# Up projections of a decoder trunk: the last product into the first accumulator with both operand parts at once, and a group's first two weight blocks rounded together

## The chip, the cores and the metric

The kernel runs on one core of one Trainium2 chip (trn2). The metric is the device time of one execution in microseconds; the figure given for a kernel is the median of its runs. A profiled execution has its own time, which stands beside its span (first to last instruction).

The engines in the profile: PE (TensorE, the matrix products; PEld are its weight loads), DVE (VectorE), ACT (ScalarE), POOL (GpSimd) and SP (SyncE, which issues most of the DMAs). Each has a queue of its own that it works off in order.

## The reference

A decoder layer with two feed-forward networks (FFNs) around a mixer, on a sequence of 512 positions with a model width of 1024. Only the FFNs matter here:

```python
D_MODEL = 1024
SEQ = 512
D_FF = 2816

def swiglu(x, w_gate, w_up, w_down):
    return (jax.nn.silu(x @ w_gate) * (x @ w_up)) @ w_down

x = x + 0.5 * swiglu(rmsnorm(x, ffn1_norm[l]), ffn1_wg[l], ffn1_wu[l], ffn1_wd[l])
x = x + hybrid_mixer(...)
x = x + 0.5 * swiglu(rmsnorm(x, ffn2_norm[l]), ffn2_wg[l], ffn2_wu[l], ffn2_wd[l])
```

Input and output are float32. The gate and up projections (`x @ w_gate`, `x @ w_up`) are what the change touches; they stand in both FFNs.

## The kernel before

**Two-part products.** PE multiplies operands rounded to a short float format (F32R). To keep float32 accuracy the kernel splits each operand into a rounded part and what the rounding leaves: `wsplit` (line 235) makes `wh` by a copy on ACT and `wl` by a subtraction on DVE. A product is then the sum of three: rounded weights with the rounded operand, rounded weights with the operand's rest, the weights' rest with the rounded operand. A moving operand `m` of 256 columns is kept as one tile of 512: `m[:, lo]` is the rounded part, `m[:, hi]` the rest.

**Fast scheme over blocks.** `ffn_up` (line 376) makes the gate and up projections. The first columns of the weights go the direct way (in the first FFN a few blocks before it as well). The rest goes through a seven-product scheme: of a two by two split of weights and operand, seven products of half size stand for eight. The weights come in groups: a *pass* `w` takes two column blocks of the gate weights (even `w`, `o.j` = 0) or of the up weights (odd `w`). The first FFN has 16 passes, the second 18 (`count`). A pass has seven steps, numbered 1 to 7 in the code (here p1 to p7), each with its own weight block of 512 columns: raw halves of the loaded tile for p1 and p2 (`o.x`), loaded blocks or sums for the others. `s2` and `s4` are sums that `add_weights` makes on DVE.

**Order of steps.** The list `stream` (line 449) sets it: in each pass p1, p2, p4 of the pass before, p6, p3 of the pass before, p5, p7. One step is one item `i` of the stream, done in this order (the loop at the end of `ffn_up`): `products(i)` on PE, `results(i - 1)` on ACT and DVE, `prepare(i + LEAD)`, which rounds the weights of four steps ahead, and DMAs for later passes. Rounded weights live in tiles of 1024 columns that hold two consecutive steps (`units`, three of each kind). Once in 14 steps, a number of times, `halve` also rounds a finished result `h` for the down projection (`hh` on ACT, `hl` on DVE): in the first FFN six times, in the second four.

**Accumulators.** Each pass has three PSUM banks: `o.beta` (tag mm) collects p1, p6, p7 and p4 in turn, `o.gamma` (tag aux) p5 and p3, `o.p2` (tag aux) p2. After p1, p6 and p7 ACT copies what stands in beta's first half to SBUF, and the next of them goes on adding into the same bank, so PE may not start it before the copy is done. `t1` and `t2` (tiles `tg` in even passes, `tu` in odd ones) collect results; `silu` runs on them in even passes, and in odd passes DVE multiplies them with those of the even pass before, into `h`.

**Wide steps.** In `products` a step is either narrow, per weight tile three products of 256 columns (rounded weights with `m[:, lo]`, with `m[:, hi]`, and the weights' rest with `m[:, lo]`), or wide, per weight tile one product of 512 columns (rounded weights with the whole of `m`, so that the two parts land in the two halves of the bank) and one of 256. A wide step leaves a second half in the bank, which DVE has to add. `wide(p, w)` (line 504) says which: before, p2, p5 and p3, from pass `FIRST_WIDE` = 2 on, p5 and p3 not in the last two passes.

**What order holds what.** ACT and DVE work off their queues in the order in which the code emits. In a step that follows p4 (that is during p6), `results` for p4 comes first, then the rounding of the block four steps ahead, which is p1 of the next pass.

The other places that the prediction names: `psum` pools of four banks for each tag; `load` (line 432) issues a pass's loads; `halve` (line 598); the calls of `ffn_up` at lines 803 and 1698. All engine calls pass through one recording line, so the profile puts every instruction at L170, and rows are told apart by tile names: `wh<-wr` and `wh<-s` are rounding copies, `wl<-...` the subtractions, `tg<-mm` and `tu<-mm` ACT's copies out of beta, `tg<-aux` and `tu<-aux` DVE's answers to p2, p5 and p3, `mm<-cm,wh` a product into beta, `aux<-cm,wh` one into the other banks.

Of the kernel before, what the change touches and what calls it, by code (L numbers as in the profile page):

```python
# [9 lines left out]
F32 = mybir.dt.float32  # L10
F32R = mybir.dt.float32r
AF = mybir.ActivationFunctionType
# [31 lines left out]
LEAD = 4  # L44
PLAIN, PAIRS, TAIL = 6, 8, 3
DIRECT = 4
WIDE, FIRST_WIDE = (2, 5, 3), 2


ORDER = """  # L50
# [125 lines left out]
def hybrid_kernel(ctx, tc, xt, vec, w1u, w1d, wm, wki, wrg, watt, wrnn, wout, w2u, w2d, gf, out):  # L176
    nc = tc.nc
    plan = Plan()
    V, A = plan.engine("DVE", nc.vector), plan.engine("ACT", nc.scalar)
# [18 lines left out]
    def nm(s):  # L198
        cnt[0] += 1
        return f"{s}_{cnt[0]}"  # L200

    def slot(dt=F32, name="s"):
        return plan.take("slot", big.tile([P, S], dt, tag="slot", name=nm(name)))

    def work(name="t", cols=S):
        return plan.take("tmp", tmp.tile([P, cols], F32, tag="tmp", name=nm(name)))

    def awork(name="a"):
        return patt.tile([P, S], F32, tag="att", name=nm(name))

    def psum(tag="mm"):
        return psp.tile([P, S], F32, tag=tag, name=nm(tag))
# [22 lines left out]
    def wsplit(r, h, l):  # L235
        A.activation(h, r, AF.Copy)
        V.tensor_sub(l, r, f(h))
# [75 lines left out]
    lo, hi = slice(0, HS), slice(HS, S)  # L313
# [62 lines left out]
    def ffn_up(y, wu, n0, hs, g, waiting=(), given=(), ahead=None):  # L376
# [10 lines left out]
        ws = []  # L387
# [65 lines left out]
        w = count - 1  # L453
        stream[-3:] = [(5, w), (7, w), (3, w - 1), (4, w), (3, w)]
        units = []

        def add_weights(i):
            p, w = stream[i] if i < len(stream) else (0, 0)
            o = ws[w]
            if p == 6:  # L460
                o.s2 = slot(F32, "s2")
                V.tensor_add(o.s2, o.s1, o.x[:, :H])
            if p == 3:
                o.s4 = slot(F32, "s4")
                V.tensor_add(o.s4, o.s2, o.x[:, H:])

        def prepare(i):
            if i < LEAD:
                add_weights(i)
            if i + 1 >= LEAD:  # L470
                add_weights(i + 1)
            p, w = stream[i]
            o = ws[w]
            if i % 2 == 0:
                units.append([wsp.tile([P, WMAX], F32R, tag=t, name=nm(t)) for t in ("wh", "wl")])
            h, l = (t[:, i % 2 * H:(i % 2 + 1) * H] for t in units[i // 2])
            wsplit({1: lambda: o.x[:, :H], 2: lambda: o.x[:, H:], 6: lambda: o.s2, 5: lambda: o.s1, 7: lambda: o.s3,
                    4: lambda: o.a22, 3: lambda: o.s4}[p](), h, l)
# [25 lines left out]
        def wide(p, w):  # L504

            return p in WIDE and FIRST_WIDE <= w < count - 2 * (p != 2)

        def results(i):
            p, w = stream[i]
            o = ws[w]  # L510
            if p == 1:
                o.t1, o.t2 = (work("tg"), work("tg")) if o.j == 0 else (awork("tu"), awork("tu"))
                A.activation(o.t1[:, lo], o.beta[:, lo], AF.Copy)
            elif p == 2:
                V.tensor_sub(o.t1[:, lo], o.p2[:, lo], o.t1[:, lo])
                if wide(2, w):
                    V.tensor_add(o.t1[:, lo], o.p2[:, hi], o.t1[:, lo])
            elif p == 6:
                A.activation(o.t1[:, hi], o.beta[:, lo], AF.Copy)
            elif p == 7:  # L520
                A.activation(o.t2[:, hi], o.beta[:, lo], AF.Copy)
                V.tensor_add(o.t2[:, hi], o.gamma[:, lo], o.t2[:, hi])
                if wide(5, w):
                    V.tensor_add(o.t2[:, hi], o.gamma[:, hi], o.t2[:, hi])
                if o.j:
                    o.h2 = slot(F32, "h")
                    V.tensor_mul(o.h2[:, hi], o.t2[:, hi], ws[w - 1].t2[:, hi])
                else:
                    A.activation(o.t2[:, hi], o.t2[:, hi], AF.Silu)
            elif p == 4:  # L530
                if o.j:
                    V.tensor_mul(o.h2[:, lo], o.beta[:, lo], ws[w - 1].t2[:, lo])
                else:
                    A.activation(o.t2[:, lo], o.beta[:, lo], AF.Silu)
            elif p == 3:
                V.scalar_tensor_tensor(o.t1[:, hi], o.gamma[:, lo], -1.0, o.t1[:, hi], op0=ALU.mult, op1=ALU.subtract)
                if wide(3, w):
                    V.tensor_sub(o.t1[:, hi], o.t1[:, hi], o.gamma[:, hi])
                if o.j:
                    o.h1 = slot(F32, "h")  # L540
                    V.tensor_mul(o.h1, o.t1, ws[w - 1].t1)
                    hs.extend((o.h1, o.h2))
                else:
                    A.activation(o.t1, o.t1, AF.Silu)

        with tc.manual_schedule(engines=ENGINES):
# [4 lines left out]
            for d, (n, j) in enumerate(direct):  # L551
                sums.append(psum(("aux", "mm")[n % 2]))
                if d == 1:
                    norm_rest(norm)
                    hs.extend(ffn_act(*p) for p in waiting)
                gemm(sums[d], split_[d], y, range(KD), last=False, upto=KD // 2)
                steps = [results_direct(d - 1)] if d else []
                if d + 2 < len(direct):
                    together(prepare_direct(), *steps)
                    fetch()  # L560
                else:
                    together(*steps)
                    for i in range(2):
                        prepare(2 * (d + 2 - len(direct)) + i)
                if d == 0:
                    for _ in range(3):
                        next(norm)
                if d in (4, 6):
                    load_ = load(len(ws))
                if d >= 4:  # L570
                    next(load_, None)
                if d > 1:
                    next(operands, None)
                gemm(sums[d], split_[d], y, range(KD), first=False, since=KD // 2)
                if d > 1:
                    next(operands, None)
            for _ in operands:
                pass
            for i in range(len(stream)):
                products(i)  # L580
                if i:
                    results(i - 1)
                else:
                    together(results_direct(len(direct) - 1))
                if i + LEAD < len(stream):
                    prepare(i + LEAD)
                elif not ahead or i + LEAD - len(stream) < PLAIN - f0:
                    halve(hs, f0 + i + LEAD - len(stream))
                if ahead:
                    ahead(i - len(stream))  # L590
                if i % 14 == 12 and i // 14 < f0:
                    halve(hs, i // 14)
                if i % 7 == 1 and len(ws) < count:
                    load_ = load(len(ws))
                next(load_, None)
            results(len(stream) - 1)

    def halve(hs, n):
# [182 lines left out]
    def given(r):  # L781
        h, l = (wsp.tile([P, WMAX], F32R, tag=t, name=nm(t)) for t in ("wh", "wl"))
        wsplit(r, h, l)
        return h, l
# [10 lines left out]
    pu, w = psum(), given(AH[0])  # L795
# [779 lines left out]
    steps, index, units, turned, tasks_at = d2.steps, d2.index, d2.units, d2.turned, d2.tasks_at  # L1575
# [211 lines left out]
```

## Time and profile before

| | us |
|---|---|
| median of three runs | 1067.38 (1066.7 to 1067.38) |
| the profiled execution | 1067.44 |
| its span | 1065.6 |
| PE busy | 1056.1 |
| DVE busy | 879.8 |
| ACT busy | 652.8 |
| POOL busy | 155.8 |

How to read the rows. A row of the timeline has start and length in us from the start of the span, then engine, line, operation, the tile written and those read, shapes, and how many equal rows were merged (x2); in brackets the engine's idle time before it and who ended it. Lengths of consecutive rows on ACT and DVE overlap, since one starts before the last has written everything; what an engine can take is therefore read from start to start. Matmuls overlap in the same way. In the windows each engine has its busy us in that stretch and in brackets its instructions. The chain is followed back from the last instruction of the program.

The product streams lie at about 74 to 235 us (first FFN) and 765 to 945 us (second).

### The profile page before, as it was taken

How to read it: one execution, taken by the hardware profiler on the slowest of the kernel's cores; microseconds unless marked ns; L12 is line 12 of the kernel's file. 1: busy time of each engine (PE TensorE's matmuls, PEld its weight loads, DVE VectorE, ACT ScalarE, POOL GpSimd, SP SyncE). 2: the span in 40 equal slices, each digit the busy share in tenths (PEclk: the TensorE clock that was granted, in tenths of full speed). 3: DMA queues.
4: the chain of work that ended last, by engine and by line, in shares of the span. 5: the costliest groups of instructions: out<-in, count | busy, mean ns of one | idle time of the engine just before them, and what ended most of it. 6: DMA issues, size and time to landing. Idle time of an engine off the chain costs nothing.

```text
span 1065.6 us, 17037 instructions
## 1 busy us (share of the span) xinstructions
PE 1056.1 (99%) x6084; PEld 929.0 (87%) x6084; DVE 879.8 (83%) x1734; ACT 652.8 (61%) x1295; POOL 155.8 (15%) x187
## 2 busy tenths in 40 slices
PE   9999999999999999999999999999999999999997
PEld 7889999999999888888888888888899999998885
DVE  6687898889978889898989866766878988878885
ACT  6575555556656669867796573446655555565753
POOL 0161111102430000000000000001511111101610
PEclk9999999999999999999999999999999999999999
DMA  8298777738983442232223212434977786638973
GB/s 278 60 260 190 162 200 182 179 109 236 262 197 105 146 134 79 85 109 80 83 76 99 80 41 59 139 111 113 245 190 164 190 198 162 163 120 255 256 160 119
DMA packets 71701, 161.77 MB, mean 152 GB/s; under 512 B 8512, under 2 KB 14784, under 8 KB 71616
## 3 DMA queue, kind: packets, MB, share of 16 engines
q1 hardware_dynamic: 46608, 119.72, 34.8%
q0 software_dynamic: 24576, 40.38, 23.0%
q8 instruction: 48, 0.79, 0.3%
q10 hardware_dynamic: 432, 0.57, 0.1%
q14 instruction: 37, 0.30, 0.1%
HBM read 151.73 MB, written 2.10 MB: 144 GB/s over the span
## 4 chain that ended last, share of the span: by engine, by line
PE 94%; DVE 3%; ACT 2%; issue 1%; DMA 0%; SPq 0%; ACTq 0%
PE mm L170 66%; PE aux L170 28%; DVE wl L170 1%; ACT wh L170 1%; DVE ca L170 1%; DMA x<-xt 0%; ACT cm L170 0%; DVE h L170 0%; DVE cb L170 0%; DVE tg L170 0%; ACT tg L170 0%; DVE cm L170 0%; ACT yh L170 0%; SPq L158 0%; DVE o L170 0%
## 5 line engine op out<-in xcount | busy, mean ns | idle before, releaser
L170 PE MATMUL mm<-cm,wh 128*128 128x256 f32 x1472 | 268.5, 283 | 0.1
L170 PEld LDWEIGHTS mm<-cm,wh 128*128 128x128 f32 x1472 | 229.1, 191 | 3.5 <-ACT tg L170 0.3
L170 DVE TENSOR_TENSOR wl<-wr,wh 128x512 fp32r<-128x512 f32 (+2 forms) x228 | 188.7, 831 | 49.6 <-ACT wh L170 48.0
L170 ACT ACTIVATE wh<-wr 128x512 fp32r<-128x512 f32 (+3 forms) x230 | 167.9, 737 | 68.8 <-PE mm L170 23.4
L170 PE MATMUL mm<-cm,wl 128*128 128x256 f32 x736 | 208.4, 283 | 0.0
L170 PE MATMUL mm<-yh,wh 128*128 128x512 f32 (+1 forms) x416 | 164.0, 395 | 0.8 <-ACT wh L170 0.8
L170 PE MATMUL mm<-yl,wh 128*128 128x512 f32 (+1 forms) x416 | 162.3, 391 | 0.1
L170 PE MATMUL mm<-yh,wl 128*128 128x512 f32 x408 | 159.3, 390 | 0.0
L170 PE MATMUL aux<-cm,wh 128*128 128x512 f32 (+1 forms) x552 | 159.2, 351 | 0.0
L170 PEld LDWEIGHTS mm<-cm,wl 128*128 128x128 f32 x736 | 140.4, 191 | 0.0
L170 ACT ACTIVATE wh<-s 128x512 fp32r<-128x512 f32 x152 | 92.9, 624 | 54.3 <-DVE s L170 41.8
L170 DVE TENSOR_TENSOR wl<-s,wh 128x512 fp32r<-128x512 f32 x152 | 103.5, 686 | 24.9 <-ACT wh L170 23.2
L170 PE MATMUL aux<-cm,wl 128*128 128x256 f32 x440 | 123.8, 281 | 0.0
L170 PEld LDWEIGHTS aux<-cm,wh 128*128 128x128 f32 x552 | 96.6, 189 | 12.5
L170 PEld LDWEIGHTS mm<-yh,wh 128*128 128x128 f32 (+1 forms) x416 | 77.9, 187 | 17.6 <-ACT wh L170 1.4
L170 PEld LDWEIGHTS mm<-yl,wh 128*128 128x128 f32 (+1 forms) x416 | 77.6, 187 | 15.7 <-DVE yl L170 0.8
L170 PEld LDWEIGHTS mm<-yh,wl 128*128 128x128 f32 x408 | 76.6, 188 | 16.6 <-DVE wl L170 0.2
L170 PEld LDWEIGHTS aux<-cm,wl 128*128 128x128 f32 x440 | 83.5, 190 | 0.0
L170 PE MATMUL mm<-wh,cm 128*128 128x512 f32 x192 | 59.0, 389 | 0.0
L170 ACT ACTIVATE tg<-tg 128x512 f32<-128x512 f32 (+1 forms) x44 | 24.1, 548 | 50.8 <-DVE tg L170 50.7
L158 POOL DMA_DIRECT2D cm<-cb x8 | 7.1, 884 | 320.4 <-PE mm L170 265.6
L158 POOL DMA_DIRECT2D s<-w2u x36 | 33.5, 1063 | 125.9 <-DMA s<-w2u 42.2
(243 smaller groups left out, 2049.5 us busy)
## 6 DMA issues: line engine op xcount, KB each, us to landing
wr<-wm SPq DMA_DIRECT2D x39, 512.0 KB, 3.6
wr<-w2u SPq DMA_DIRECT2D x26, 512.0 KB, 5.1
wr<-w1u SPq DMA_DIRECT2D x21, 512.0 KB, 5.6
wr<-w1d SPq DMA_DIRECT2D x18, 512.0 KB, 4.7
s<-w2u SPq DMA_DIRECT2D x36, 256.0 KB, 5.9
s<-w2u POOLq DMA_DIRECT2D x36, 256.0 KB, 5.3
wr<-w2d SPq DMA_DIRECT2D x18, 512.0 KB, 5.6
s<-w1u SPq DMA_DIRECT2D x32, 256.0 KB, 5.9
```

The costliest lines, as they stand in the source:

```text
L158: return self.engine.dma_start(out, src, **kw)
L170: return call(*args, **kw)
```

## The change

Two things, in both FFNs.

First, p4 becomes a wide step in passes 2 to `count` - 3. Its product with rounded weights covers both operand parts and lands in both halves of `beta`. `results` for such a p4 copies beta's first half to t2 on ACT, adds the second half on DVE, and only then finishes t2 as a whole: in an odd pass one product of 512 columns into `h`, in an even pass one `silu` over 512 columns. What p7's results did to t2's second half (a product of 256 or a silu of 256) is left out there.

Second, where p1 falls on an even step, which is so in pass 0 and every even pass, its block and p2's, the two halves of the loaded tile `o.x`, are rounded by one call of `wsplit` over 1024 columns when p1's turn comes, and p2's turn does nothing.

```diff
-WIDE, FIRST_WIDE = (2, 5, 3), 2
+WIDE, FIRST_WIDE = (2, 5, 3, 4), 2
...
                 units.append([wsp.tile([P, WMAX], F32R, tag=t, name=nm(t)) for t in ("wh", "wl")])
+            if p == 1 and i % 2 == 0:
+
+                wsplit(o.x, *units[i // 2])
+                return
+            if p == 2 and i % 2:
+                return
             h, l = (t[:, i % 2 * H:(i % 2 + 1) * H] for t in units[i // 2])
...
                 if wide(5, w):
                     V.tensor_add(o.t2[:, hi], o.gamma[:, hi], o.t2[:, hi])
+                if wide(4, w):
+                    return
                 if o.j:
                     o.h2 = slot(F32, "h")
                     V.tensor_mul(o.h2[:, hi], o.t2[:, hi], ws[w - 1].t2[:, hi])
                 else:
                     A.activation(o.t2[:, hi], o.t2[:, hi], AF.Silu)
+            elif p == 4 and wide(4, w):
+                A.activation(o.t2[:, lo], o.beta[:, lo], AF.Copy)
+                V.tensor_add(o.t2[:, lo], o.beta[:, hi], o.t2[:, lo])
+                if o.j:
+                    o.h2 = slot(F32, "h")
+                    V.tensor_mul(o.h2, o.t2, ws[w - 1].t2)
+                else:
+                    A.activation(o.t2, o.t2, AF.Silu)
             elif p == 4:
                 if o.j:
                     V.tensor_mul(o.h2[:, lo], o.beta[:, lo], ws[w - 1].t2[:, lo])
```

## The prediction

> **What bounds the kernel now.** I read the page first: its busy times and the shares of the chain that ended last.
>
> ```profile
> span 1065.6 us, 17037 instructions
> PE 1056.1 (99%) x6084; PEld 929.0 (87%) x6084; DVE 879.8 (83%) x1734; ACT 652.8 (61%) x1295; POOL 155.8 (15%) x187
> PE 94%; DVE 3%; ACT 2%; issue 1%; DMA 0%; SPq 0%; ACTq 0%
> ```
>
> PE is busy nearly throughout and carries 94% of the chain. Next I asked the chain for a stretch inside the product stream of the first FFN, the only kind of place that the change touches. Columns are start, length, what ran.
>
> ```profile
> 114.54 2.88 PE mm L170 x24
> ...
> 123.11 1.41 PE aux L170 x8
> ...
> 134.51 2.88 PE mm L170 x24
> ```
>
> Here every step is PE. A block of twelve 128x256 products takes 2.88 / 2 = 1.44 us, a wide one (four 128x512 and four 128x256) 1.41 us. A pass of the stream has seven blocks; two passes take 134.51 - 114.54 = 19.97 us, which is 8 x 1.44 + 6 x 1.41 = 19.98, so PE loses nothing. Who is next? The windows (busy us of each engine) and the timelines of DVE, ACT and PE in one pair of passes tell.
>
> ```profile
> 130.00:160.00 30.00, 30.00 (x218) 28.36 (x217) 27.11 (x53) 17.93 (x37) 5.96 (x7) 1.00 0.71 184
> ```
>
> ```profile
> 120.52 0.69 DVE L170 TENSOR_TENSOR s<-s,wr 128x512 f32<-128x512 f32 x1
> 121.12 0.69 DVE L170 TENSOR_TENSOR wl<-a,wh 128x512 fp32r<-128x512 f32 x1
> ...
> 122.92 0.88 DVE L170 TENSOR_TENSOR tg<-aux,tg 128x256 f32<-128x256 f32 x2
> 124.81 1.48 DVE L170 TENSOR_TENSOR wl<-s,wh 128x512 fp32r<-128x512 f32 x2 [1.01 <-ACT wh L170]
> 126.21 0.88 DVE L170 TENSOR_TENSOR tu<-aux,tu 128x256 f32<-128x256 f32 x2
> 127.00 0.68 DVE L170 TENSOR_TENSOR wl<-s,wh 128x512 fp32r<-128x512 f32 x1
> 127.60 1.47 DVE L170 TENSOR_TENSOR wl<-wr,wh 128x512 fp32r<-128x512 f32 x2
> 128.99 0.42 DVE L170 SCALAR_TENSOR_TENSOR tg<-aux,tg 128x256 f32<-128x256 f32 x1
> 129.44 0.42 DVE L170 TENSOR_TENSOR tg<-tg,aux 128x256 f32<-128x256 f32 x1
> 129.78 0.69 DVE L170 TENSOR_TENSOR s<-s,wr 128x512 f32<-128x512 f32 x1
> 131.08 0.69 DVE L170 TENSOR_TENSOR wl<-a,wh 128x512 fp32r<-128x512 f32 x1 [0.62 <-ACT wh L170]
> ```
>
> ```profile
> 123.83 0.42 ACT L170 ACTIVATE tg<-tg 128x256 f32<-128x256 f32 x1 [1.61 <-DVE tg L170]
> ...
> 126.00 0.38 ACT L170 ACTIVATE tg<-mm 128x256 f32<-128x256 f32 x1
> 126.28 0.62 ACT L170 ACTIVATE wh<-wr 128x512 fp32r<-128x512 f32 x1
> 127.44 0.39 ACT L170 ACTIVATE tu<-mm 128x256 f32<-128x256 f32 x1 [0.54 <-PE mm L170]
> ...
> 129.89 0.63 ACT L170 ACTIVATE tg<-tg 128x512 f32<-128x512 f32 x1 [1.55 <-DVE tg L170]
> 130.43 0.61 ACT L170 ACTIVATE wh<-a 128x512 fp32r<-128x512 f32 x1
> ```
>
> ```profile
> 122.95 0.40 PE L170 MATMUL aux<-cm,wh 128*128 128x512 f32 x1
> ...
> 130.06 0.40 PE L170 MATMUL mm<-cm,wh 128*128 128x256 f32 x2
> ```
>
> DVE is 90% busy (27.11 of 30), and it follows: block p2 of this pass begins at 122.95 and its answer, tu<-aux, at 126.21, 3.26 us later. DVE runs its rows strictly in order, so a row that waits holds all behind it.
>
> **DVE's budget per pair of passes, before.** Spacings, start to start: a 512 row 0.60 us (120.52 to 121.12); two dependent 256 rows 0.79 (126.21 to 127.00); a 256 row 0.45 if the next needs it (128.99 to 129.44), else 0.34 (129.44 to 129.78). From the code a pair holds 14 roundings (8.40), four sums of weights (2.40), two pairs on t1's first half (1.58), on t2's second half 0.79 and 1.24 (the odd pass adds a product), the odd pass's product with t2's first half 0.34, on t1's second half 0.79 and, with the odd pass's 512 product, 1.50, and one rounding of an earlier h (0.60): 17.64. To that come two waits that recur every pair, since DVE feeds ACT's silu and then waits for the rounding copy behind it: before 124.81, 124.81 - 122.92 - 0.79 = 1.10; before 131.08, 131.08 - 129.78 - 0.60 = 0.70. Together 19.44, against PE's 19.97. DVE has 0.53 us to spare per pair, not the 10% that its busy share suggests.
>
> **The change part by part.** *Wide p4 on PE.* It applies to passes 2 to count-3: 12 of 16 in the first FFN, 14 of 18 in the second. Each turns a 1.44 block into a 1.41 block: 26 x 0.03 = 0.78 us less. That is all that PE can gain.
>
> *The extra add and the longer product (DVE).* The beta bank now has a second half to be added. Even pass: one 256 row, 0.34 more. Odd pass: 0.45 for the add plus 0.60 for one 512 product, in place of 0.34 and 0.45 for two 256 ones: 0.26 more.
>
> *Silu of t2 moves.* Before, the even pass ran silu on t2's second half between DVE's adds and the p3 rounding, which is the 1.10 wait; that goes. Its first half came straight from the bank (tg<-mm, 126.00) and asked nothing of DVE. Now ACT copies the half out, waits for DVE's add, runs silu over 512, and only then does the next rounding copy, for which DVE waits. Queued behind ACT's silu are that rounding and then tu<-mm (127.44), the copy that empties the next pass's bank.
>
> *Merged rounding.* In every even pass's p1 and p2 one 1024 copy and one 1024 subtraction stand for two of 512. The direct products already have such rows:
>
> ```profile
> 744.32 1.04 ACT L170 ACTIVATE wh<-wr 128x1024 fp32r<-128x1024 f32 x1
> 745.27 0.71 ACT L170 ACTIVATE cm<-ca 128x256 fp32r<-128x256 f32 x2
> ...
> 745.39 1.23 DVE L170 TENSOR_TENSOR wl<-wr,wh 128x1024 fp32r<-128x1024 f32 x1 [0.53 <-ACT wh L170]
> 746.54 0.68 DVE L170 TENSOR_TENSOR h<-h,tg 128x512 f32<-128x512 f32 x1
> ```
>
> DVE: 746.54 - 745.39 = 1.15 for 1.20, 0.05 less. But the subtraction starts 745.39 - 744.32 = 1.07 after the copy starts, a 512 one 131.08 - 130.43 = 0.65 after it: 0.42 more waiting. The merge falls in the very step where ACT runs the moved silu, because an even pass's p1 is prepared four blocks ahead, in p6 of the odd pass, right behind results of p4.
>
> The Trainium skill (Perfetto Trace Analysis, Optimizing Scalar/DVE Operations) says that larger operations can raise throughput when the engine is saturated, and that splitting them can end work sooner when the engine is not saturated but others wait for it. The rows show both at once, -0.05 busy and +0.42 waiting, so by the first half of that rule alone the pair would come out 0.42 us shorter than below.
>
> *Sum for DVE after.* Busy: 17.64 + 0.34 + 0.26 - 0.05 = 18.19. Waits: the 0.70 stays; the 1.10 goes; new, from the add's start to the 1024 subtraction: add 0.42, 0.03 until silu (129.44 + 0.42 = 129.86, silu at 129.89), 0.54 until the copy (129.89 to 130.43), 1.07 until the subtraction, less the 0.34 that DVE spends on the add itself: 1.72. Total 20.61, against PE's 19.97 - 0.06 = 19.91. DVE now falls behind by 0.70 per pair; without the h rounding (made for six pairs in the first FFN, four in the second) by 0.10. Unmerged, the same sum gives 18.24 + 0.70 + 1.30 = 20.24.
>
> *Where PE feels it.* Block p7 of an odd pass overwrites the bank that tu<-mm empties. Now that copy ends at 127.44 + 0.39 = 127.83, and p7 starts at 130.06: 2.23 to spare. After, with DVE as punctual as now: add at 127.60 (where DVE is free), silu 128.05, copy of 1024 at 128.59, tu<-mm at 129.54 (0.95 later, 744.32 to 745.27), done 129.93, against 130.03. So the slack is gone before DVE is late at all. The first pairs are better off, as DVE starts ahead:
>
> ```profile
> 794.10 0.40 PE L170 MATMUL aux<-cm,wh 128*128 128x512 f32 x1
> ...
> 796.87 0.88 DVE L170 TENSOR_TENSOR tu<-aux,tu 128x256 f32<-128x256 f32 x2
> ```
>
> In pass 3 the answer to p2 comes after 2.77 us, not 3.26, and the lost 1.10 wait helps once. I set the changed order out row by row with these spacings from pass 0 (the old order set out so answers p2 after 2.72 in pass 3 and 3.20 in pass 5, and PE never waits). Spare time at p7: 1.35 in pass 3, 0.58 in pass 5, then none. PE waits 0.31 in the third pair (0.22 at p7 of pass 7, 0.09 at the next p6), and from then on about what DVE loses, 0.67 to 0.76. First FFN, six pairs: 0.31 + 0.76 + 0.76 + 0.67 = 2.50. Second, seven pairs, the last three without the h rounding: 0.31 + 0.67 + 3 x 0.16 = 1.46. Loss 3.96, gain 0.78: +3.2 us.
>
> DMA issues keep their order on both queues, and weights are fetched a pass ahead; I cost that at nothing (bound: one late landing, which would show as a wait of ACT's copy for a DMA). The down projections start with DVE about 1.5 us later than now but with blocks of plain products rounded four blocks ahead, so nothing there; without that cover, up to 1.5 per FFN, 3.0.
>
> **The number.** The profiled execution took 1067.44 us around its span of 1065.6; the median shown is 1067.38, the same to 0.01%. 1067.4 + 3.2 = 1070.6. The spacings are known to about 1.5%. Short by that, DVE's 18.19 loses 0.27 per pair, and the layout ends at +1.2; long by it, at +5.8. So this case's own range is 1068.6 to 1073.2.
>
> **Rivals.** *The cover holds.* If DVE and ACT overlap a little better than laid out, PE never waits and the wide block alone counts: 1067.4 - 0.8 = 1066.6. For it: the first two pairs need it anyway, and 0.10 per pair decides in the second FFN. Against: the 1.72 wait is a chain of measured rows. It decides if DVE's pair stays under 19.91, 0.70 less than my sum.
>
> *DVE behind from the first pair.* If nothing is gained at the start and the h rounding does not matter, all 13 pairs lose 0.70: +9.1 - 0.8, 1075.7. Against it: the 2.77 above.
>
> *The weight loads count.* The change drops 4 of 12 loads per block. If PE were paced by loads, at 1.44 / 12 = 0.12 us each, 26 x 0.48 = 12.5 us would go and the kernel would take 1054.9. The rows speak against it: wide blocks already drop those loads and take 1.41, not 0.96. The Trainium skill (TensorE: Matmul & The Clock Gate, Back-to-back issue gap) has 131 ns per N=512 product in a sustained stream; by that, as an estimate, a wide block takes 4 x 0.131 + 4 x 0.12 = 1.00 us and the change saves 26 x 0.44 = 11.4 us; the trace, with its 1.41, does not agree.
>
> **Chances.** Forecast 54%, cover holds 32%, DVE behind from the start 11%, weight loads 3%. What a measurement of this kernel can tell from no change is 0.2%, 2.1 us: faster means below 1065.3, slower above 1069.5. The forecast gives slower in 46 of its 54, the rest no change; cover holds gives no change; so faster 3%, same 40%, slower 57%. The range goes from 1066.3, just under the cover case, to 1074.6, above the long-spacing end and short of the last rival.
>
> **What would show it.** Right: PE's waits list gains ACT's tu copy (PE mm behind ACT tu) with some ten waits under 0.8 us, all in the stream's later passes; passes of a pair take 20.6 us there in the first FFN, about 20.1 late in the second; DVE waits about 1.7 us before the 1024 subtraction; blocks of p4 take 1.41. Wrong: PE gapless at 19.91 per pair (cover holds), or gaps from pass 3 on, or waits of PE for wl rather than for the bank.

## The result, and the profile after

| | before | after |
|---|---|---|
| median (us) | 1067.02 (1066.37 to 1067.38, 6 runs) | 1071.17 (1070.95 to 1071.75, 6 runs) |
| ratio, 95% interval | | 1.0039 [1.0029, 1.005] |
| span of the profiled execution (us) | 1065.6 | 1069.3 |

The change makes the kernel 4.15 us slower. The page of the kernel after, its span, its busy times and the shares of the chain:

```profile
span 1069.3 us, 16812 instructions
PE 1058.2 (99%) x5980; PEld 923.7 (86%) x5980; DVE 883.4 (83%) x1730; ACT 653.6 (61%) x1291; POOL 154.3 (14%) x187
PE 96%; ACT 1%; DVE 1%; issue 1%; DMA 0%; SPq 0%; DVEq 0%; ACTq 0%
```

There are 104 products fewer (26 steps times 4), as the change says, and no share of busy time tells where the loss is: PE reads 99% and DVE 83% in both. PE's list of waits (total us, times, longest) does:

```profile
PE mm L170 <- ACT tu L170: 1.4, 4, 0.4
PE aux L170 <- DVE epst L170: 1.1, 1, 1.1
PE aux L170 <- DVE tu L170: 1.0, 1, 1.0
PE aux L170 <- DVE acc L170: 0.2, 1, 0.2
```

The second and the fourth line stand in the list of before too. The first and the third are new: short waits for ACT's copy out of beta, and one long one for DVE. To see what each costs I divided both traces at the starts of PE's products: where each stream begins and ends, and where the second down projection has its opening part behind it (its first product with an operand of tag cm). Lengths in us; the last columns are kernels of the experiments below.

| stretch | before | after | one region | wide alone | silu later |
|---|---|---|---|---|---|
| up to the first stream | 73.80 | 73.15 | 73.11 | 73.50 | 72.85 |
| first stream | 160.54 | 162.77 | 162.81 | 161.78 | 160.32 |
| first down projection | 113.39 | 113.40 | 113.39 | 113.39 | 113.39 |
| between the FFNs | 417.65 | 417.62 | 417.63 | 417.74 | 417.63 |
| second stream | 180.86 | 182.02 | 182.03 | 181.11 | 180.64 |
| opening of the second down projection | 19.21 | 20.41 | 19.30 | 19.41 | 19.21 |
| rest | 100.19 | 99.94 | 99.93 | 99.88 | 99.91 |

Three stretches account for the loss: +2.23 in the first stream, +1.16 in the second, +1.20 behind it. Together they are 4.59; the first and the last row are 0.90 shorter, which leaves the 3.69 between the two spans. These two rows move from kernel to kernel where nothing was changed, the first by up to 0.95 and the last by up to 0.31 in the table, so I read nothing from them.

**The streams.** Around one late event of the first stream, DVE, ACT and PE of the kernel after:

```profile
185.85 1.28 DVE L170 TENSOR_TENSOR wl<-s,wh 128x512 fp32r<-128x512 f32 x2
187.05 0.88 DVE L170 TENSOR_TENSOR tu<-aux,tu 128x256 f32<-128x256 f32 x2
...
188.44 0.42 DVE L170 TENSOR_TENSOR tg<-mm,tg 128x256 f32<-128x256 f32 x1
190.51 1.23 DVE L170 TENSOR_TENSOR wl<-wr,wh 128x1024 fp32r<-128x1024 f32 x1 [1.65 <-ACT wh L170]
```

```profile
188.89 0.63 ACT L170 ACTIVATE tg<-tg 128x512 f32<-128x512 f32 x1 [2.10 <-DVE tg L170]
189.43 1.04 ACT L170 ACTIVATE wh<-wr 128x1024 fp32r<-128x1024 f32 x1
190.38 0.36 ACT L170 ACTIVATE tu<-mm 128x256 f32<-128x256 f32 x1
```

```profile
190.16 0.28 PE L170 MATMUL aux<-cm,wl 128*128 128x256 f32 x1
190.79 0.50 PE L170 MATMUL mm<-cm,wh 128*128 128x256 f32 x2 [0.35 <-ACT tu L170]
191.13 0.28 PE L170 MATMUL mm<-cm,wl 128*128 128x256 f32 x1
```

The reader is to follow one thread through the three. DVE adds p4's second half at 188.44. ACT's silu, which needs that sum, starts at 188.89; the rounding copy queued behind it at 189.43; DVE's subtraction, which needs the copy, at 190.51. Behind the same copy ACT has tu<-mm, which empties the bank that p7 is to write. It ends at 190.38 + 0.36 = 190.74, and p7 starts at 190.79, 0.63 behind the last product before it where 0.12 is usual. How often this happens shows in the chain, at the starts of p7 in the odd passes:

```profile
170.12 3.14 PE mm L170 x24
...
190.79 3.14 PE mm L170 x24
...
211.47 3.12 PE mm L170 x24
```

They are 20.67 and 20.68 us apart: that is a pair of passes now, against 19.97 before. In the second stream pairs are 20.68 while an `h` is rounded in them, and 20.07 or 20.08 later.

**Behind the second stream.** The long wait. ACT, DVE and PE of the kernel after at the end of the stream:

```profile
948.81 0.38 ACT L170 ACTIVATE xr<-mm 128x256 f32<-128x256 f32 x1 [2.75 <-PE mm L170]
949.09 0.63 ACT L170 ACTIVATE tg<-tg 128x512 f32<-128x512 f32 x1
949.62 1.14 ACT L170 ACTIVATE wh<-wr 128x512 fp32r<-128x512 f32 x2
```

```profile
950.27 0.69 DVE L170 TENSOR_TENSOR wl<-wr,wh 128x512 fp32r<-128x512 f32 x1 [2.30 <-ACT wh L170]
...
951.81 0.42 DVE L170 SCALAR_TENSOR_TENSOR tu<-aux,tu 128x256 f32<-128x256 f32 x1
```

```profile
939.54 0.49 PE L170 MATMUL mm<-ident,x 128*128 128x128 f32 x3
...
948.50 0.71 PE L170 MATMUL mm<-ident,x 128*128 128x128 f32 x5
...
952.28 0.50 PE L170 MATMUL aux<-wh,hh 128*128 128x512 f32 x1 [1.00 <-DVE tu L170]
```

The rows mm<-ident are transposes that belong to the down projection. In the kernel before, PE runs eight of them in a row behind the stream's last product, and ACT copies their results in one go:

```profile
945.44 1.03 PE L170 MATMUL mm<-ident,x 128*128 128x128 f32 x8
```

```profile
946.08 1.21 ACT L170 ACTIVATE xr<-mm 128x256 f32<-128x256 f32 x4 [0.21 <-PE mm L170]
```

In the kernel after, three of the eight run at 939.54, inside the stream, and ACT's first copy of their results, xr<-mm, stands in its queue ahead of the last silu, tg<-tg. That copy waits until PE comes to the other transposes at 948.50; silu, two rounding copies and DVE's work wait with it, and a bank that DVE has to read out comes free only at 952.2, 1.00 us late for PE. In the code of the changed kernel nothing is moved there: the stream and the down projection are two regions of hand-set order, and at the border between them the framework's scheduler orders the instructions by itself.

### The profile page after: what moved, and what is told of

Read it like the earlier page. It is cut to its first block, busy times and chain, and to the rows that moved or that the text cites. A ratio compares the mean times of both kernels' runs of the same rounds, so it can differ in the third digit from the quotient of the medians.

```text
span 1069.3 us, 16812 instructions
## 1 busy us (share of the span) xinstructions
PE 1058.2 (99%) x5980; PEld 923.7 (86%) x5980; DVE 883.4 (83%) x1730; ACT 653.6 (61%) x1291; POOL 154.3 (14%) x187
## 4 chain that ended last, share of the span: by engine, by line
PE 96%; ACT 1%; DVE 1%; issue 1%; DMA 0%; SPq 0%; DVEq 0%; ACTq 0%
PE mm L170 68%; PE aux L170 28%; ACT wh L170 1%; DMA x<-xt 0%; DVE wl L170 0%; ACT yh L170 0%; SPq L158 0%; DVE o L170 0%; DVE tg L170 0%; ACT tu L170 0%; DVE yl L170 0%; DVE xr L170 0%; DVE acc L170 0%; DVE sq L170 0%; ACT sq L170 0%
## 5 line engine op out<-in xcount | busy, mean ns | idle before, releaser
L170 PE MATMUL mm<-cm,wh 128*128 128x256 f32 (+1 forms) x1368 | 269.1, 293 | 1.5 <-ACT tu L170 1.4
L170 DVE TENSOR_TENSOR wl<-wr,wh 128x512 fp32r<-128x512 f32 (+2 forms) x211 | 185.2, 886 | 65.6 <-ACT wh L170 65.1
L170 PEld LDWEIGHTS mm<-cm,wh 128*128 128x128 f32 x1368 | 216.4, 191 | 12.4 <-ACT tu L170 4.0
L170 ACT ACTIVATE wh<-wr 128x512 fp32r<-128x512 f32 (+3 forms) x213 | 164.6, 780 | 69.8 <-PE mm L170 23.4
L170 ACT ACTIVATE tg<-tg 128x512 f32<-128x512 f32 (+1 forms) x44 | 26.9, 611 | 54.9 <-DVE tg L170 54.9
```

What stands on the lines that cost most here:

```text
L170: return call(*args, **kw)
```

## The experiments

**The border: one region around the stream and the down projection.** Everything else as in the kernel after.

```diff
+    with tc.manual_schedule(engines=ENGINES):
         ffn_up(y2, w2u, 0, hs, V_G2, ahead=tasks_at)
         with tc.manual_schedule(engines=ENGINES):
...
```

> The changed kernel, with the second FFN's product stream and its down projection ordered as one region, so that the first transposes of the down projection and ACT's copies of them stand behind the stream's last rows again, as they did before the change. Nothing else differs. Theory: the loss has two parts, DVE behind in the streams (+2.2 us in the first, +1.2 us in the second) and one wait of 1.0 us at the second down projection that comes from the changed order at the seam. Then this kernel takes 1070.1 us or a little less, the waits in the streams stay, and no PE wait of 1 us is left at the seam. Rival: the wait at the seam is DVE's lag of the stream, paid late; then it stays about 1.0 us and the time about 1071.2.

Measured 1070.09 us (1069.96 to 1070.36), 1.0029 [1.0018, 1.0041] of before. ACT's queue at the same place:

```profile
947.99 0.63 ACT L170 ACTIVATE tg<-tg 128x512 f32<-128x512 f32 x1 [1.95 <-DVE tg L170]
948.52 1.14 ACT L170 ACTIVATE wh<-wr 128x512 fp32r<-128x512 f32 x2
949.57 1.19 ACT L170 ACTIVATE xr<-mm 128x256 f32<-128x256 f32 x4
```

The silu is again ahead of the copies. In PE's list of waits the 1.0 us line is gone, the one for ACT's tu copy is still there with 1.4 us in 4 waits, and the opening takes 19.30 instead of 20.41: 1.1 of the 4.15 us came from the border. The streams are as they were (162.81 and 182.03). Why the scheduler moved the transposes in the kernel after and not in the one before wasn't tried.

**The wide step alone.** The two conditions in `prepare` for the merged rounding are taken out; with the one region, so compare with the run above.

```diff
-            if p == 1 and i % 2 == 0:
-
-                wsplit(o.x, *units[i // 2])
-                return
-            if p == 2 and i % 2:
-                return
```

> The wide p4 alone: the first two blocks are rounded one by one again; the seam ordered as one region. Theory (DVE's pair 20.24 us against PE's 19.91 while an h is rounded, 19.64 without): the first stream 1.1 us longer than before, the second about 0.1 shorter, so 1068.1 us, with PE waits of 0.2 to 0.4 us from pass 9 on in the first stream. Rival (the merged rounding helps, the wide p4 alone costs all): 1070 or more. Rival (the extra add is hidden): 1066.3.

Measured 1067.99 us (1067.7 to 1069.24), 1.0011 [1.0002, 1.002] of before, 2.1 us less than with the merge. ACT and DVE of this kernel at the event that was shown for the kernel after:

```profile
188.58 0.63 ACT L170 ACTIVATE tg<-tg 128x512 f32<-128x512 f32 x1 [2.11 <-DVE tg L170]
189.12 0.61 ACT L170 ACTIVATE wh<-wr 128x512 fp32r<-128x512 f32 x1
189.64 0.36 ACT L170 ACTIVATE tu<-mm 128x256 f32<-128x256 f32 x1
189.90 0.62 ACT L170 ACTIVATE wh<-wr 128x512 fp32r<-128x512 f32 x1
```

```profile
188.13 0.42 DVE L170 TENSOR_TENSOR tg<-mm,tg 128x256 f32<-128x256 f32 x1
189.76 1.48 DVE L170 TENSOR_TENSOR wl<-wr,wh 128x512 fp32r<-128x512 f32 x2 [1.22 <-ACT wh L170]
```

Two things are better than with the merge. DVE waits 1.22, and inside the row of two (which takes 1.40 to the next row, not 1.20) another 0.20, instead of 1.65. And tu<-mm now stands between the two copies, so it follows the start of the first by 0.52, not by 0.95. No wait of PE for it is listed any more; DVE and ACT still fall behind, only later: counted from p2 of the odd passes, pairs of the first stream take 19.95 up to pass 9, then 20.38 and 20.50, and the chain then goes through ACT's copy tg<-mm into p6. The forecast's sum for this pair was 20.24; the 0.20 inside the row of two isn't in that sum. The first stream is 1.24 longer than before, where 1.1 was expected. In the second, where the `h` rounding stops early, little is lost: 181.11 is 0.25 over the kernel before, where 0.1 under it was expected.

**The merge alone.** p4 narrow as before.

```diff
-WIDE, FIRST_WIDE = (2, 5, 3, 4), 2
+WIDE, FIRST_WIDE = (2, 5, 3), 2
```

> The merged rounding alone: p4 stays narrow everywhere, p1 and p2 of the even passes are rounded together. Theory: without silu in front of it the longer copy lies beside other work, PE does not wait in the streams, and the time is that of the kernel before, 1067.0 us within 0.5. Rival: the later first block costs by itself, 1068 or more, with PE waits for wl at p1.

Measured 1066.7 us, 0.9998 [0.9989, 1.0007] of before. The merge by itself costs nothing that these runs can tell: its streams take 160.51 and 180.85 in the trace, those of before 160.54 and 180.86. Its rows, ACT and then DVE:

```profile
185.66 1.05 ACT L170 ACTIVATE wh<-wr 128x1024 fp32r<-128x1024 f32 x1
```

```profile
186.98 1.22 DVE L170 TENSOR_TENSOR wl<-wr,wh 128x1024 fp32r<-128x1024 f32 x1
```

Without a silu ahead of it the copy starts 1.32 us before DVE comes to the subtraction, and the subtraction waits for nothing. So the 2.1 us above belong to the two parts together: the longer copy hurt only where it started behind the moved silu.

**The silu later.** The kernel after, with the even pass's silu of t2 emitted behind the rounding of the next block instead of ahead of it.

```diff
                     V.tensor_mul(o.h2, o.t2, ws[w - 1].t2)
-                else:
-                    A.activation(o.t2, o.t2, AF.Silu)
...
                     halve(hs, f0 + i + LEAD - len(stream))
+                p, w = stream[i - 1]
+                if i and p == 4 and wide(4, w) and not ws[w].j:
+                    A.activation(ws[w].t2, ws[w].t2, AF.Silu)
```

> The changed kernel, with one row moved: in the even passes the silu over 512 columns of t2 stands on ACT behind the rounding copy of p1 and not in front of it. The work is the same. Theory (what costs is not DVE's 0.55 us more work per pair but its wait for add, silu and copy in a row, 1.72 us): the wait shrinks to that for the copy alone, DVE's pair is under 19 us, PE never waits in the streams and keeps its 0.78 us: 1066.3 us. Rival (DVE's added work is what costs): about as slow as the changed kernel, 1070 or more.

Measured 1066.22 us (1065.57 to 1067.24, 11 runs), 0.9994 [0.9985, 1.0003] of before: the whole loss is gone, with the extra add, the longer product and the merge all still there. This kernel has no region added, and yet the border came out in the order of the kernel before (19.21 in the table), so the move took both losses away at once; for the streams alone compare the two kernels with one region, 1070.09 us above and 1066.51 below. DVE and ACT at the same event:

```profile
185.23 0.42 DVE L170 TENSOR_TENSOR tg<-mm,tg 128x256 f32<-128x256 f32 x1
186.18 1.22 DVE L170 TENSOR_TENSOR wl<-wr,wh 128x1024 fp32r<-128x1024 f32 x1 [0.52 <-ACT wh L170]
187.66 0.42 DVE L170 SCALAR_TENSOR_TENSOR tg<-aux,tg 128x256 f32<-128x256 f32 x1 [0.26 <-PE aux L170]
```

```profile
184.81 0.38 ACT L170 ACTIVATE tg<-mm 128x256 f32<-128x256 f32 x1 [1.41 <-PE mm L170]
185.09 1.05 ACT L170 ACTIVATE wh<-wr 128x1024 fp32r<-128x1024 f32 x1
186.04 0.62 ACT L170 ACTIVATE tg<-tg 128x512 f32<-128x512 f32 x1
186.56 0.37 ACT L170 ACTIVATE tu<-mm 128x256 f32<-128x256 f32 x1
```

The copy no longer asks for DVE's add, so DVE's wait falls from 1.65 to 0.52, tu<-mm is done at 186.56 + 0.37 = 186.93, and p7 starts at 188.88, 1.95 us later. The last DVE row waits for PE: DVE has caught up. The same two blocks of the chain a pair apart, and a block with the wide p4 in it:

```profile
102.17 1.41 PE aux L170 x8
103.57 2.85 PE mm L170 x20
...
122.10 1.41 PE aux L170 x8
```

The 20 products from 103.57 on are a narrow step and the wide p4, 2.85 where the kernel before has 24 products and 2.88. A pair is 122.10 - 102.17 = 19.93 here and 19.95 in most others, against 19.97; the streams are 160.32 and 180.64 long, 0.22 each under before. That is the whole of the gain of the change, 0.44 us, once nothing waits.

Two variants of it, one with the one region added and one with that and without the merge, where the late silu stands behind p1's copy alone:

> The kernel with the moved silu again, seam ordered as one region (its order of rows is the same without that). Same as before it: 1066.2 us, streams 0.2 us shorter each than in the kernel before, pairs of passes 19.95 us against 19.98. A second sample for whether it beats the kernel before.

> The wide p4 alone (no merged rounding), with silu of t2 behind the rounding copy of p1 on ACT, seam as one region. Theory: neither PE nor DVE waits more than before; the same time as the kernel with the moved silu and the merged rounding, 1066.2 us within 0.3. Rival (the merged rounding gives something of its own once silu is out of its way): slower than that kernel by 0.5 us or more.

Measured 1066.51 (1066.18 to 1067.48), 0.9997 [0.9988, 1.0006], and 1066.37 (1065.78 to 1067.23), 0.9993 [0.9984, 1.0002]. The streams take 160.32 and 180.64, and 160.36 and 180.64: with and without the merge, the pairs between the first and the last are 19.93 to 19.95. All three kernels lie 0.3 to 0.6 us under their before, and none of the intervals excludes 1. They beat the kernel after clearly, and the one before not measurably.

**How much DVE has to spare.** The kernel before (with the one region), and in every even pass from 2 to `count` - 3 the sum `s4` written twice, or three times, with the same values: plain DVE work with no new wait.

```diff
                 o.s4 = slot(F32, "s4")
-                V.tensor_add(o.s4, o.s2, o.x[:, H:])
+                for _ in range(2 if w % 2 == 0 and FIRST_WIDE <= w < count - 2 else 1):
+                    V.tensor_add(o.s4, o.s2, o.x[:, H:])
```

> The kernel before (seam as one region), with one row of DVE done twice in each even pass from 2 to count-3: the sum s4, 128x512, is written again with the same values. 0.60 us more for DVE per pair, no new wait, PE unchanged. By the prediction's budget DVE's pair goes from 19.44 to 20.04 against PE's 19.97: 0.07 late per pair, which the 2.2 us to spare at p7 swallow, so 1066.8 us, no change. By the rows laid out one after another there is a wait of about 0.25 us per pair that the budget leaves out: PE waits 0.3 us per pair at p6 of the odd passes, from pass 7 on, +1.5 us, 1068.3. Rival (DVE has its busy share's 10% free): 1066.8 and no wait of PE at all, here and in the next run.

> The same with the sum done three times: 1.20 us more for DVE per pair. Budget 20.64 against 19.97: 0.67 late per pair, some +2 to +4 us after the slack is used up. Laid out: PE waits 0.9 us per pair at p6 of the odd passes from pass 5 on (0.4 where no h is rounded), +8.5 us, 1075.3. Rival (10% of DVE is free): 1066.8.

Measured 1070.17 us (1.0031 [1.002, 1.0041]) and 1079.64 (1.0118 [1.0104, 1.0131]): both dearer than expected, by 1.9 and 4.3 us even against the forecast that lays the rows out one after another. The opening behind the second stream takes 19.21 in both, as in the kernel before, so the loss doesn't come from the added region. One more row of 0.60 us in 20 us of an engine that reads 90% busy costs 3.4 us in all. DVE of the kernel with two sums, over one pair of passes:

```profile
180.51 0.69 DVE L170 TENSOR_TENSOR h<-tu,tg 128x512 f32<-128x512 f32 x1
...
182.32 1.41 DVE L170 TENSOR_TENSOR s<-s,wr 128x512 f32<-128x512 f32 x2
183.65 0.69 DVE L170 TENSOR_TENSOR wl<-s,wh 128x512 fp32r<-128x512 f32 x1
...
186.14 1.48 DVE L170 TENSOR_TENSOR wl<-s,wh 128x512 fp32r<-128x512 f32 x2 [1.01 <-ACT wh L170]
...
192.22 0.69 DVE L170 TENSOR_TENSOR wl<-a,wh 128x512 fp32r<-128x512 f32 x1 [0.62 <-ACT wh L170]
...
200.93 0.69 DVE L170 TENSOR_TENSOR h<-tu,tg 128x512 f32<-128x512 f32 x1
```

DVE is the clock now: 200.93 - 180.51 = 20.42 us from one `h` to the next, with no listed wait but the two that recur. The two sums take 183.65 - 182.32 = 1.33, so with the usual 0.60 for the first the second one costs 0.73 (it rewrites the tile that the first has just written). DVE's own pair without it is then 20.42 - 0.73 = 19.69, and three sums ought to give 19.69 + 1.46 = 21.15. PE's pairs in that kernel are just so long, 195.24 - 174.09 = 21.15, in its chain:

```profile
174.09 2.87 PE mm L170 x24
...
195.24 2.88 PE mm L170 x24
```

So DVE of the kernel before has 19.97 - 19.69 = 0.28 us to spare per pair with an `h` rounded, where the budget had 0.53. Taking the `h` rounding away buys less than its 0.60: 20.06 to 20.10 and 20.83 per pair without it.

## Why the prediction was right, and where it wasn't

- *DVE falls behind, 20.61 per pair in place of 19.44.* The sum for after holds: pairs take 20.67, and 20.07 without the `h` rounding (20.01 forecast). The new wait, by the forecast's own count from the add to the subtraction, is 190.51 - 188.44 - 0.34 = 1.73, against 1.72.
- *PE feels it at p7 of the odd passes, through tu<-mm.* Shown by the rows at 190.38 and 190.79, and by the silu put later, which takes both away. The third pair is the first with a loss, as laid out: 0.27 and 0.36 over 19.95, counted from the even and from the odd pass on, then 0.72. Of that, 0.51 is p7's wait, about 0.1 its slow first products (190.79 to 191.13 is 0.34, where 0.24 is usual), and a further tenth goes at the next p6.
- *2.50 and 1.46 us, less 0.78.* Measured against the streams with no waits (160.32, 180.64), the losses are 2.45 and 1.38.
- *The wide p4 gains 0.03 a block.* Mis-sized: 0.44 us over 26 blocks, 0.017 each. The price took p2's 1.41 over to p4. From its first product to the first of the next block, p4 takes 1.44 in the kernel before and 1.42 wide, in the kernel with the silu later; there p3 and p5 also take 0.005 and 0.010 longer than before, p6 and p7 0.005 and 0.004 less. Why a wide p4 takes 0.01 longer than a wide p2 wasn't tried. The weight loads didn't count: with them as the pace the block would have taken 0.96. The 1.00 us that the estimate by the Trainium skill (TensorE: Matmul & The Clock Gate, Back-to-back issue gap) gave doesn't show in any row; in a wide block the product behind one of 512 columns starts 0.24 after it (188.16 to 188.40, silu later).
- *Nothing at the down projections' start.* This is the step that failed. It holds for the first FFN (113.40 against 113.39), not for the second: 1.20 us. The working asked only whether DVE would be late there, and its bound of 1.5 per FFN stood for that; what came was another order of instructions at the border of two regions, which the kernel with one region shows. The change moved three transposes and a copy that its diff doesn't name.
- *DVE's spare 0.53 before.* Too much; the padded kernels leave 0.28. The budget counted a merged pair of subtractions as 1.20 us, while its own quoted rows put 1.40 between 124.81 and 126.21: the second subtraction has a short wait for its copy inside the merged row. That is 0.20 of the 0.25; the last 0.05 is about what the sum for after falls short by too. In the kernel after that pair is a plain 1.20 (the row of two at 185.85 has no wait), so the forecast for after wasn't touched by the 0.20. It did matter for the rival that the cover holds: that had more room in the budget than in the kernel.
- *What would show it.* The list of waits names ACT's tu copy 4 times with 1.4 us, not ten times. It counts only idle time beyond the modelled end of a matmul (0.28 us long, 0.12 apart), so waits of a tenth are not in it; the pair lengths, from start to start, were the better sign.

The forecast's 1070.6 lies 0.6 under the median, and its +3.2 at the low end of the measured interval (+3.1 to +5.3). The streams' part was right for the reason given, 3.18 forecast and 3.39 measured with the gain taken off. That the whole comes as near is partly luck: the missed 1.2 at the border was made up for in part by a start at 1067.4, 0.4 above the median of before over six runs, and by the stretches that nobody changed. With the missed 1.2, the 0.34 too much gain and the start put right the forecast would be 1071.8, 0.6 over the median; the stretches that were not changed moved by more than that in the profiled executions (-0.65 and -0.25), so the rest is not explained further.

On the merge, the Trainium skill's rule (Perfetto Trace Analysis, Optimizing Scalar/DVE Operations), larger operations for a saturated engine and split ones where others wait, comes out here on its second half: busy 83% or 90%, yet 2.1 us were lost by merging behind the silu, and nothing where the copy had time.

## What to carry to other kernels

Before a step moves to another queue position, write down what then stands behind it on that in-order engine and which bank or buffer that work sets free; here one silu, 0.54 us on an engine that is 61% busy, cost 3.6 us ahead of a merged rounding copy (1070.09 against 1066.51, both with one region), 1.6 us ahead of a single one (1067.99 against 1066.37, the same without the merge), and nothing measurable behind it. An engine's room per loop turn is the loop's length less its rows *and* the waits that recur, and a padded copy of the kernel measures it in one run. Compare the order of instructions of both kernels to the very end, borders of hand-ordered regions included.

## What was not expected

A product that starts after a wait of PE is slower at first: the rows at 190.79 and 952.28 read 0.50 where others of their kind read 0.40, and at 190.79 the next follows 0.10 later than usual, so a short wait costs about a tenth more than its idle time. The wait need not be the only reason: in the kernel before, the first product behind the eight transposes, at 946.23, reads 0.47 without a wait. The DVE row that rewrote a tile just written cost 0.73 from start to start instead of 0.60. And the framework's scheduler, given work on both sides of a border, placed transposes nine microseconds ahead of their use, with a copy that blocked ACT's queue for 2.75 us.
